# A hybrid attention and convolution step on one core: pacing of decode work, the engine of four weight halves, and two queue positions

## Chip, cores and metric

The kernel runs on one core of a Trainium2 chip. The metric is the device time of one execution in microseconds (us), and a median over several runs stands for a kernel. The engines are TensorE (PE, matmuls; PEld its weight loads), VectorE (DVE), ScalarE (ACT), GpSimd (POOL) and SyncE (SP, which here issues the DMAs). Each works through its own instructions in order and waits for others by semaphores.

## What is computed

One inference step of a two-layer trunk, for a prompt of 1024 rows of 1024 numbers and for 8 sample rows, which have their past K and V in 32 pages of 128 rows each. Everything is fp32.

```python
def ab_mix(x, ...):                         # layer 0
    q, k, v, g_a, u_b, g_b = split(x @ w_in)
    o_a = stick_breaking(q, [past; k], [past; v])   # sigmoid(z) * product of (1 - sigmoid) of later keys
    o_b = multiscale_pool(u_b) 
    return concat(o_a * silu(g_a), o_b * silu(g_b)) @ w_out

def c_mix(x, ...):                          # layer 1
    a, a_gate, gate = split(x @ w_in)
    c = depthwise_conv(a * sigmoid(a_gate), 31 taps)
    c = silu(layer_norm(c + b_dw))
    return (c * silu(gate)) @ w_out

x = layer_norm(ALPHA * x + ab_mix(x))       # then the same with c_mix
```

New K, V and the new pooling and convolution states are outputs too.

## The kernel before

**Numbers in two halves.** Each operand of a large matmul is split into a high part, rounded to the matmul's type (`whi`, `xh`, made by ACT), and the rest (`wlo`, `xl`, made by DVE or POOL as a subtraction). A product is three matmuls: high times high, low times high, high times low. `dma_w` (L198) loads a raw piece of a weight, `conv_w` (L203 to 211) makes its two halves: ACT copies at L205, and at L210 POOL subtracts, or DVE if the argument `eng` says so.

**Stages.** A setup transposes the inputs (L562) and the small weights (`setup_small`, L479: bias row, depthwise weights at L512, norm vectors). Then comes the input projection of layer 0, mixed with the attention of the prompt rows: 48 units (a head pair with a block of queries) with scores on PE, sigmoids on ACT, a scan and a product on DVE (L365 to 371), and the weighted sum on PE; the pooling groups are woven in between. Out layer 0 follows (`out_layer`, L1041): the output projection in 32 items of 24 matmuls, an item being a quarter of the columns (n4) for one block of 128 rows (tb), with the items (0, 0..3), (1, 0..3), (0, 4..7), (1, 4..7) first and the quarters 2 and 3 after. Each item is evacuated by DVE (L1067, L1071). A block that has all its quarters is normalized (L1009 DVE, L1025 ACT, L1026 POOL), and transposed by PE for the next layer (L1138). Layer 1 has its projection, the convolution (taps on DVE, ACT, POOL and PE), the conv norm and then out layer 1, again `out_layer`. The decode of V and the sample rows' small products run beside layer 1's work.

**The order** of the work of PE, ACT, DVE and POOL is the order in which the program is written; generators weave stages into each other. SP's order is made by the framework, which may move a DMA that depends on nothing. `decode_k` is a generator that scores the sample rows against their K pages. Each of its units loads two pages (L405), multiplies them with the query on POOL (three of four) or DVE (L417), and sums over a head on DVE (L409). After the 64 units of each half of the samples comes a tail: transposes and sigmoids (L429), a scan over 1024 columns (L437), a carry row (L441 to L451), scaling (L454), and transposes back (L463). `tick(n)` advances it by n steps. In attention a unit gets `TBASE + TSLOPE * (384 - n) / 384` ticks; what is left is spread over out layer 0, one tick after each item.

**Weights in out layer 0.** The first quarter's four pieces are ready before the layer; the second quarter's four are made in its first four steps, as `convs` says, with POOL for the even ones and DVE for the odd ones in layer 0 (L1059).

**Conv norm in layer 1.** `stats_3` (L1547) fills a queue, `midq`, in five steps `mid(0)` to `mid(4)` over the eight row blocks (1, 1, 2, 2 and 2 of them): PE broadcasts mean and scale by transposes (`mid_a`, L1569), and DVE subtracts and multiplies (`mid_b`, L1581), two operations of 128x1024 for a block. A SiLU group on ACT follows (`silus`, L1595), in two halves that are entries of the same queue, then the product with the gate (`mid_g`, L1602, DVE for blocks 3, 5 and 7, else POOL), and the split (`mid_c`: L195, L196). `midpop(EARLY)` takes three entries from the queue ahead of out layer 1; a `mid_g` takes entries until its SiLU group is out. `AT` places the rest: `mid_g(4)` at item (1, 1) of out layer 1, `mid_c(4)` at (1, 3). The sample row's norm stands beside it (L1230 to L1233, then PE's transposes L1208).

Of the kernel before, what the change touches and what calls it, by code (L numbers as in the profile page):

```python
# [65 lines left out]
WRB = 3  # L66
ETICK = 0.35
EDVE = (1, 2, 3, 0)
TBASE = 2.35
TSLOPE = 1.5  # L70
NHEADS = (0, 6, 6, 6, 6, 6, 6, 6)
SNY = 7
# [10 lines left out]
FASTB = (7,)  # L83
# [17 lines left out]
def kernel(  # L101
# [9 lines left out]
    pe, act, dve, gp, sp = nc.tensor, nc.scalar, nc.vector, nc.gpsimd, nc.sync  # L111
# [34 lines left out]
    def trp():  # L146
        return pz[0].tile([P, 512], F32, tag="zt", name="zt", bufs=NZT[0])
# [55 lines left out]
    def conv_w(raw, a, n, pool=None, eng=None, tags=("whi", "wlo"), bufs=4):  # L203
        hi = (pool or wpa).tile([P, a, n], F32R, tag=tags[0], name="whi", bufs=bufs)
        act.activation(out=hi, in_=raw, func=AF.Copy)  # L205
        if tags[1] == "kp":
            lo = pool.tile([P, 513], F32R, tag="kp", name="wlo", bufs=bufs)[:, 0:a * n].rearrange("p (k f) -> p k f", k=a)
        else:
            lo = (pool or wpa).tile([P, a, n], F32R, tag=tags[1], name="wlo", bufs=bufs)
        (eng or gp).tensor_tensor(out=lo, in0=raw, in1=hi.bitcast(F32), op=ALU.subtract)  # L210
        return hi, lo
# [259 lines left out]
    def tick(n):  # L471
        while n > 0 and queue:
            try:
                next(queue[0])
                n -= 1
            except StopIteration:
                queue.pop(0)
# [454 lines left out]
    queue.append(decode_k())  # L932
    small_gen = setup_small()
    fill = Filler(blocks_gen(blocks, CHUNKS, qw[0], when=WCONVA, lead=WLEAD))
    ecred = 0.0
    while ("v0", 2) not in fill.seen:
        fill.part()
        next(small_gen, None)
        if ("k0", 2) in fill.seen and (0, 0) not in SQ:
            prep(0, 0)  # L940
        ecred += ETICK
        tick(int(ecred))
        ecred -= int(ecred)
# [3 lines left out]
    for u in range(len(units) + 2):  # L947
        if u < len(units):
# [6 lines left out]
            fcred += fbase  # L955
            tcred += TBASE + TSLOPE * (384 - n) / 384.0
            z_a(u)
# [80 lines left out]
    def out_layer(w, first, ahead, X, gb, pool, finish, between, before=None, half=None, tail=None, lag=OLAG, fast0=FAST, wide=0, gps=()):  # L1038
        order = [(n4, tb) for t0 in (0, 4) for n4 in range(2) for tb in range(t0, t0 + 4)]
        for i in range(NTB + lag):  # L1040
            if i < NTB:  # L1041
                order.append((2, i))
            if i >= lag:
                order.append((3, i - lag))
        dmas = {0: (1, 3)} | {9 + i: (2, i) for i in range(4)} | {13 + i: (3, i) for i in range(4)}
        convs = {i: (1, i) for i in range(4)} | {12 + i: (2, i) for i in range(4)} | {16 + i: (3, i) for i in range(4)}
        raws, sts = {}, {}
        tiles = {0: first, 1: [], 2: [], 3: []}

        def fetch(q, i):  # L1050
            raws[q, i] = dma_quarter(w, q, i)

        for i in range(3):
            raws[1, i] = ahead[i]
        for s, (n4, tb) in enumerate(order):
            f0 = n4 * 256
            if s in convs:
                q, i = convs[s]
                tiles[q].append(conv_w(raws[q, i], 2, 256, pool if q % 2 else None, dve if q == 1 and i % 2 and fast0 is FASTB else None))  # L1059
            if s in dmas:  # L1060
                fetch(*dmas[s])
            if before is not None:
                before(n4, tb)
            o = (trp() if s < wide and s % 3 else acc())[:, 0:256]
            out_group(tiles[n4], o, tb, half)
            y = X[tb]
            dve.scalar_tensor_tensor(out=y[:, f0:f0 + 256], in0=y[:, f0:f0 + 256], scalar=ALPHA,  # L1067
                                     in1=o, op0=ALU.mult, op1=ALU.add)
            if n4 == 0:
                sts[tb] = pool.tile([P, 4, 6], F32, tag="st", name="st", bufs=NTB)  # L1070
            dve.bn_stats(sts[tb][:, n4, :], y[:, f0:f0 + 256])  # L1071
            if n4 == 3:
                fast = tb in fast0
                halves = (slice(0, 512), slice(512, 1024)) if tb >= 6 else (slice(0, 1024),)
                mv, rs = norm_s(pool, sts[tb])

                def app(y=y, mv=mv, rs=rs, tb=tb, fast=fast, halves=halves):
                    if fast and gps:
                        hs = (slice(0, 512), slice(512, 1024))
                        bs = [norm_fast(gb[0], y, mv, rs, h, i, gps) for i, h in enumerate(hs)]  # L1080
                        for h, b in zip(hs, bs):
                            b()
                            finish(tb, y, h)
                        return
                    norm_a(gb[0], y, mv, halves, gps)
                    for h in halves:
                        norm_b(gb[0], y, rs, fast, h)
                        finish(tb, y, h)
                defer((DTC if fast0 is FASTB else DTD)[tb], app)
            between(n4, tb)  # L1090
            point()
            if tail is not None:
                tail(n4, tb)
# [432 lines left out]
    MID = ((0, 1), (1, 2), (2, 4), (4, 6), (6, 8))  # L1526
# [19 lines left out]
        defer(4, stats_3)  # L1546

    def stats_3():
        for c in range(len(MID)):
            midq.append(lambda c=c: (mid_a(c), mid_b(c)))  # L1550
            if c < 2:
                silus(c)
        silus(2)
        reached.append(1)

    midq = []
# [6 lines left out]
    def mid_a(c):  # L1563
        a, b = MID[c]
        if c == 0:
            BC["wide"] = pz[0].tile([P, S], F32, tag="conv", name="rows", bufs=1)
        t = BC["wide"][:, c * 512:c * 512 + 512] if c < 2 else trp()
        for i, tb in enumerate(range(a, b)):
            pe.transpose(out=t[:, i * P:(i + 1) * P], in_=rmf[:, tb:tb + 1].broadcast_to([P, P]), identity=ident)  # L1569
            pe.transpose(out=t[:, 256 + i * P:256 + (i + 1) * P], in_=rvf[:, tb:tb + 1].broadcast_to([P, P]),  # L1570
                         identity=ident)
        BC[c] = t

    def mid_b(c):
        a, b = MID[c]
        t = BC[c]
        for i, tb in enumerate(range(a, b)):
            cc = C[:, tb]
            for o0, op in ((0, ALU.subtract), (256, ALU.mult)):
                bc = t[:, o0 + i * P:o0 + (i + 1) * P].rearrange("p (o c) -> p o c", o=1).broadcast_to([P, NK, P])  # L1580
                dve.tensor_tensor(out=cc, in0=cc, in1=bc, op=op)  # L1581
# [3 lines left out]
    def silus(c):  # L1585
        for i in range(SPLIT):
            midq.append(lambda i=i: mid_s(c, i))
# [71 lines left out]
    fill.part(1)  # L1659
    tick(1)  # L1660
    mid_c(1)
    for c in range(3, len(MID)):
        silus(c)
    midpop(EARLY)
    fill.part(1)
    tick(1)
# [36 lines left out]
```

## Time and profile before

| what | value |
|---|---|
| median of 3 runs | 1110.16 us (1109.91 to 1115.74) |
| profiled execution | 1110.31 us |
| its span in the profile | 1108.5 us |
| mean granted clock of PE | 0.972 |
| busy: PE, DVE, POOL, ACT | 1042.0, 833.3, 632.2, 493.4 us |

The profile shows one execution. A span is some 1.8 us shorter than the time of the execution, which has a start and an end around it. A row of a timeline gives the start, the busy time, the engine, the line, the operation with what it writes and reads, and in brackets how long the engine was idle before and what released it. A stage's row gives the busy time of each engine within it.

### The profile page before, as it was taken

How to read it: one execution, taken by the hardware profiler on the slowest of the kernel's cores; microseconds unless marked ns; L12 is line 12 of the kernel's file. 1: busy time of each engine (PE TensorE's matmuls, PEld its weight loads, DVE VectorE, ACT ScalarE, POOL GpSimd, SP SyncE). 2: the span in 40 equal slices, each digit the busy share in tenths (PEclk: the TensorE clock that was granted, in tenths of full speed). 3: DMA queues.
4: the chain of work that ended last, by engine and by line, in shares of the span. 5: the costliest groups of instructions: out<-in, count | busy, mean ns of one | idle time of the engine just before them, and what ended most of it. 6: DMA issues, size and time to landing. Idle time of an engine off the chain costs nothing.

```text
span 1108.5 us, 19858 instructions
## 1 busy us (share of the span) xinstructions
PE 1042.0 (94%) x6804; PEld 840.1 (76%) x6804; DVE 833.3 (75%) x982; ACT 493.4 (45%) x933; POOL 632.2 (57%) x488
## 2 busy tenths in 40 slices
PE   8899998999999989979988999999999899799996
PEld 7897887888888878979986666566666466678786
DVE  3368899899689988698874699999999960584246
ACT  5245665665766647601143244534543412462111
POOL 3266858567276878568765266757764612342135
PEclk9999999999999989989988999999999999889998
DMA  8577857865457776478425786877687678386933
GB/s 268 171 205 228 253 181 214 257 207 176 131 158 230 243 217 217 151 263 267 155 100 177 218 262 214 267 241 232 208 263 235 205 244 266 111 271 217 321 108 135
DMA packets 179350, 235.20 MB, mean 212 GB/s; under 512 B 15434, under 2 KB 95955, under 8 KB 179225
## 3 DMA queue, kind: packets, MB, share of 16 engines
q1 hardware_dynamic: 179249, 233.94, 67.0%
q8 instruction: 53, 0.87, 0.3%
q14 instruction: 48, 0.39, 0.1%
HBM read 212.60 MB, written 16.14 MB: 206 GB/s over the span
## 4 chain that ended last, share of the span: by engine, by line
PE 51%; POOL 7%; DVE 6%; DMA 5%; issue 2%; ACT 2%; SPq 2%; POOLq 0%; DVEq 0%; ACTq 0%
PE acc L225 10%; PE acc L227 9%; PE acc L226 9%; PE qv L1163 6%; DMA kt<-in_cache_k_dram 3%; POOL kt L417 2%; PE acc L1034 2%; PE acc L1036 2%; PE acc L1035 2%; DVE conv L1581 2%; PE zt L1034 1%; POOL wlo L210 1%; DVE xl L196 1%; PE qv L1199 1%; PE zt L1035 1%
## 5 line engine op out<-in xcount | busy, mean ns | idle before, releaser
L225 PE MATMUL acc<-xh,whi 128*128 128x384 f32 (+2 forms) x960 | 360.3, 375 | 1.9 <-DVE hbt L705 1.4
L227 PE MATMUL acc<-xl,whi 128*128 128x384 f32 (+2 forms) x960 | 339.3, 353 | 0.5 <-DVE xl L196 0.5
L226 PE MATMUL acc<-xh,wlo 128*128 128x384 f32 (+2 forms) x960 | 338.8, 353 | 0.0
L417 POOL TENSOR_TENSOR kt<-kt,qbs 128x1024 f32<-128x1024 f32 x96 | 237.8, 2487 | 79.0 <-DMA kt<-in_cache_k_dram 58.8
L210 POOL TENSOR_TENSOR wlo<-wraw,whi 128x512 fp32r<-128x512 f32 x122 | 163.6, 1345 | 176.6 <-ACT whi L205 154.0
L1385 DVE SCALAR_TENSOR_TENSOR conv_acc<-hbuf,wdwT,conv_acc 128x1024 f32<-128x1024 f32 x196 | 252.8, 1290 | 6.8
L225 PEld LDWEIGHTS acc<-xh,whi 128*128 128x128 f32 x960 | 183.0, 191 | 68.5 <-issue 27.2
L227 PEld LDWEIGHTS acc<-xl,whi 128*128 128x128 f32 x960 | 182.8, 190 | 18.4 <-DVE xl L196 0.9
L226 PEld LDWEIGHTS acc<-xh,wlo 128*128 128x128 f32 x960 | 183.4, 191 | 15.8
L409 DVE TENSOR_REDUCE zw<-kt 128x16 f32<-128x1024 f32 x128 | 152.9, 1211 | 28.0 <-POOL kt L417 23.0
L1375 POOL TENSOR_TENSOR conv<-conv,tap 128x512 f32<-128x512 f32 x84 | 105.9, 1293 | 15.5 <-ACT tap L1372 15.5
L205 ACT ACTIVATE whi<-wraw 128x512 fp32r<-128x512 f32 x126 | 77.6, 625 | 71.9 <-DMA wraw<-in_w_out_ab_dram 55.8
L1034 PE MATMUL acc<-whi,xh 128*128 128x256 f32 x352 | 103.9, 295 | 0.0
L1036 PE MATMUL acc<-whi,xl 128*128 128x256 f32 x352 | 101.0, 287 | 2.2 <-DVE xl L196 2.2
L1035 PE MATMUL acc<-wlo,xh 128*128 128x256 f32 x352 | 100.9, 287 | 0.6 <-POOL wlo L210 0.6
L365 DVE TENSOR_TENSOR_SCAN kp<-kp,zt 128x512 f32<-128x512 f32 (+3 forms) x96 | 92.5, 964 | 6.1 <-ACT zt L361 6.1
L1372 ACT ACTIVATE tap<-hbuf,wdwT 128x512 f32<-128x512 f32 x84 | 59.8, 721 | 46.1 <-POOL conv L1375 37.7
L1163 PE MATMUL qv<-vt,zw 128*32 128x512 f32 x512 | 74.5, 603 | 3.1 <-DMA vt<-in_cache_v_dram 3.1
L360 ACT ACTIVATE kp<-zt,nbiash 128x512 f32<-128x512 f32 (+3 forms) x96 | 55.8, 581 | 46.0 <-PE zt L823 24.5
L1034 PEld LDWEIGHTS acc<-whi,xh 128*128 128x128 f32 x352 | 68.5, 194 | 8.3 <-issue 7.8
L1036 PEld LDWEIGHTS acc<-whi,xl 128*128 128x128 f32 x352 | 68.5, 195 | 2.4 <-DVE xl L196 2.4
L1035 PEld LDWEIGHTS acc<-wlo,xh 128*128 128x128 f32 x352 | 68.5, 195 | 1.1 <-POOL wlo L210 1.0
(286 smaller groups left out, 1501.7 us busy)
## 6 DMA issues: line engine op xcount, KB each, us to landing
kt<-in_cache_k_dram SPq DMA_DIRECT2D x256, 256.0 KB
vt<-in_cache_v_dram SPq DMA_DIRECT2D x256, 256.0 KB
wraw<-in_w_in_c_dram SPq DMA_DIRECT2D x48, 256.0 KB
vt<-in_w_in_c_dram SPq DMA_DIRECT2D x48, 256.0 KB
wraw<-in_w_in_ab_dram SPq DMA_DIRECT2D x46, 256.0 KB
xt<-in_x_prompt_dram SPq DMA_DIRECT2D x8, 512.0 KB
wraw<-in_w_out_ab_dram SPq DMA_DIRECT2D x16, 256.0 KB
xres<-in_x_prompt_dram SPq DMA_DIRECT2D x8, 512.0 KB
```

Of the source, the lines that this page charges most:

```text
L210: (eng or gp).tensor_tensor(out=lo, in0=raw, in1=hi.bitcast(F32), op=ALU.subtract)
L225: pe.matmul(o, hi[:, k % 4, :], xh, start=(k == 0), stop=False)
L226: pe.matmul(o, lo[:, k % 4, :], xh, start=False, stop=False)
L227: pe.matmul(o, hi[:, k % 4, :], xl, start=False, stop=(k == NK - 1))
L409: dve.tensor_reduce(out=seg[:, j // 8, j % 8:j % 8 + 2, bi * 8:bi * 8 + 8], in_=kts.pop(s - KLAG - 1).rearrange("p a (h d) -> p a h d", d=DH),
L417: eng.tensor_tensor(out=kt, in0=kt, in1=qrow[b], op=ALU.mult)
L1034: pe.matmul(o, XH[:, k, cs], hi[:, k % 2, :], start=(k == 0), stop=False)
L1035: pe.matmul(o, XH[:, k, cs], lo[:, k % 2, :], start=False, stop=False)
L1036: pe.matmul(o, XL[:, k, cs], hi[:, k % 2, :], start=False, stop=(k == NK - 1))
L1163: pe.matmul(pv[32 * bi:32 * bi + 32, :], Z[:, j % 8 * 4 + j // 8, :], vts[bi], start=(j == 0), stop=(j == NPG - 1), tile_position=(0, 32 * ...
L1375: gp.tensor_tensor(out=ch, in0=ch, in1=tcs(t), op=ALU.add)
L1385: dve.scalar_tensor_tensor(out=part[1], in0=hb[:, j:j + S], scalar=w, in1=part[1], op0=ALU.mult, op1=ALU.add)
```

## The change

There are four edits. `TBASE` rises from 2.35 to 2.6. In the setup, the second and third advance of `setup_small` are left out, so that its later parts come two fill parts later. In out layer 0, POOL makes all low halves of the second quarter. In the conv norm, `mid(4)` is no longer queued with the others but behind the SiLU group 3.

```diff
--- before.py
+++ after.py
@@ -66,7 +66,7 @@
 WRB = 3
 ETICK = 0.35
 EDVE = (1, 2, 3, 0)
-TBASE = 2.35
+TBASE = 2.6
 TSLOPE = 1.5
 NHEADS = (0, 6, 6, 6, 6, 6, 6, 6)
 SNY = 7
@@ -932,10 +932,12 @@
     queue.append(decode_k())
     small_gen = setup_small()
     fill = Filler(blocks_gen(blocks, CHUNKS, qw[0], when=WCONVA, lead=WLEAD))
-    ecred = 0.0
+    ecred, early = 0.0, 0
     while ("v0", 2) not in fill.seen:
         fill.part()
-        next(small_gen, None)
+        early += 1
+        if early == 1 or early > 3:
+            next(small_gen, None)
         if ("k0", 2) in fill.seen and (0, 0) not in SQ:
             prep(0, 0)
         ecred += ETICK
@@ -1056,7 +1058,7 @@
             f0 = n4 * 256
             if s in convs:
                 q, i = convs[s]
-                tiles[q].append(conv_w(raws[q, i], 2, 256, pool if q % 2 else None, dve if q == 1 and i % 2 and fast0 is FASTB else None))
+                tiles[q].append(conv_w(raws[q, i], 2, 256, pool if q % 2 else None))
             if s in dmas:
                 fetch(*dmas[s])
             if before is not None:
@@ -1546,7 +1548,7 @@
         defer(4, stats_3)
 
     def stats_3():
-        for c in range(len(MID)):
+        for c in range(len(MID) - 1):
             midq.append(lambda c=c: (mid_a(c), mid_b(c)))
             if c < 2:
                 silus(c)
@@ -1659,8 +1661,9 @@
     fill.part(1)
     tick(1)
     mid_c(1)
-    for c in range(3, len(MID)):
-        silus(c)
+    silus(3)
+    midq.append(lambda: (mid_a(4), mid_b(4)))
+    silus(4)
     midpop(EARLY)
     fill.part(1)
     tick(1)
```

POOL at the start of out layer 0, behind the split of the pooled part; L210 makes the low halves of the second quarter (one row for each piece), L417 multiplies pages of K for the decode. Before:

```order
L196 TENSOR_TENSOR xl<-hs,xh 128x4x128 x4
L210 TENSOR_TENSOR wlo<-wraw,whi 128x512
L417 TENSOR_TENSOR kt<-kt,qbs 128x1024 x2
L210 TENSOR_TENSOR wlo<-wraw,whi 128x512
L417 TENSOR_TENSOR kt<-kt,qbs 128x1024 x7
```

and with the change:

```order
L196 TENSOR_TENSOR xl<-hs,xh 128x4x128 x4
L210 TENSOR_TENSOR wlo<-wraw,whi 128x512
L417 TENSOR_TENSOR kt<-kt,qbs 128x1024
L210 TENSOR_TENSOR wlo<-wraw,whi 128x512
L417 TENSOR_TENSOR kt<-kt,qbs 128x1024
L210 TENSOR_TENSOR wlo<-wraw,whi 128x512
L417 TENSOR_TENSOR kt<-kt,qbs 128x1024
L210 TENSOR_TENSOR wlo<-wraw,whi 128x512
L417 TENSOR_TENSOR kt<-kt,qbs 128x1024 x6
```

The second and fourth piece, which were on DVE, now stand on POOL, with one multiplication of K between each two.

DVE in out layer 0, around the scan of the decode tail (L437); L1067 and L1071 (L1069 and L1073 in the changed file) evacuate an item, L999, L1009 and L196 belong to the normalization and the split of finished blocks. Before:

```order
L1067 SCALAR_TENSOR_TENSOR xres<-xres,acc 128x256
L1071 BN_STATS st<-xres 128x6
L999 BN_AGGR mv<-st 128x2
L437 SCALAR_TENSOR_TENSOR kpd<-kpd 128x1024
L196 TENSOR_TENSOR xl<-zt,xh 128x4x128 x2
L1009 SCALAR_TENSOR_TENSOR xres<-xres,mv,o 128x512
L1009 SCALAR_TENSOR_TENSOR xres<-xres,mv,qv 128x512
L1067 SCALAR_TENSOR_TENSOR xres<-xres,acc 128x256
L1071 BN_STATS st<-xres 128x6
```

and with the change:

```order
L1069 SCALAR_TENSOR_TENSOR xres<-xres,acc 128x256
L1073 BN_STATS st<-xres 128x6
L1069 SCALAR_TENSOR_TENSOR xres<-xres,acc 128x256
L1073 BN_STATS st<-xres 128x6
L437 SCALAR_TENSOR_TENSOR kpd<-kpd 128x1024
L1069 SCALAR_TENSOR_TENSOR xres<-xres,acc 128x256
L1073 BN_STATS st<-xres 128x6
L1069 SCALAR_TENSOR_TENSOR xres<-xres,acc 128x256
L1073 BN_STATS st<-xres 128x6
```

The scan now stands among items of the middle of the layer, ahead of the first normalization.

DVE in out layer 1, at items (1, 1) to (1, 3); L1581 (L1583) is the conv norm's `mid_b`, L1602 (L1604) the product with the gate, L1223 to L1233 (L1225 to L1235) the sample row's norm. Before:

```order
L1223 TENSOR_SCALAR sA<-sA,zt 128x256
L1224 TENSOR_TENSOR sB<-sA 128x256
L1225 TENSOR_REDUCE small<-sB 128x1
L1602 TENSOR_TENSOR conv<-conv,gate 128x1024
L1067 SCALAR_TENSOR_TENSOR conv<-conv,zt 128x256
L1071 BN_STATS st<-conv 128x6
L1067 SCALAR_TENSOR_TENSOR conv<-conv,acc 128x256
L1071 BN_STATS st<-conv 128x6
L196 TENSOR_TENSOR xl<-conv,xh 128x8x128 x2
L1230 TENSOR_SCALAR small<-zt 128x1
L1232 SCALAR_TENSOR_TENSOR sA<-sA,small 128x256
L1233 TENSOR_TENSOR sA<-sA 128x256
```

and with the change:

```order
L1225 TENSOR_SCALAR sA<-sA,zt 128x256
L1226 TENSOR_TENSOR sB<-sA 128x256
L1227 TENSOR_REDUCE small<-sB 128x1
L1583 TENSOR_TENSOR conv<-conv,zt 128x1024 x4
L1604 TENSOR_TENSOR conv<-conv,gate 128x1024
L1069 SCALAR_TENSOR_TENSOR conv<-conv,zt 128x256
L1073 BN_STATS st<-conv 128x6
L1069 SCALAR_TENSOR_TENSOR conv<-conv,acc 128x256
L1073 BN_STATS st<-conv 128x6
L196 TENSOR_TENSOR xl<-conv,xh 128x8x128 x2
L1232 TENSOR_SCALAR small<-zt 128x1
L1234 SCALAR_TENSOR_TENSOR sA<-sA,small 128x256
```

The four operations of `mid(4)` now stand just ahead of the product with the gate. On ACT the same edit puts half a SiLU group (x4) ahead of the gate accumulator's evacuation at the start of out layer 1; before:

```order
L1595 ACTIVATE conv<-conv,pvec 128x128 x8
L205 ACTIVATE whi<-wraw 128x512 x2
L195 ACTIVATE xh<-conv 128x8x128
L1463 ACTIVATE gate<-acc 128x4x128
L205 ACTIVATE whi<-wraw 128x512 x2
L1463 ACTIVATE gate<-acc 128x4x128
L1595 ACTIVATE conv<-conv,pvec 128x2x128 x8
```

and with the change:

```order
L1597 ACTIVATE conv<-conv,pvec 128x128 x8
L205 ACTIVATE whi<-wraw 128x512 x2
L195 ACTIVATE xh<-conv 128x8x128
L1597 ACTIVATE conv<-conv,pvec 128x2x128 x4
L1465 ACTIVATE gate<-acc 128x4x128
L205 ACTIVATE whi<-wraw 128x512 x2
L1465 ACTIVATE gate<-acc 128x4x128
L1597 ACTIVATE conv<-conv,pvec 128x2x128 x4
```

The group's second half now stands behind the second evacuation. SP's order changes in one place: the copy of the conv state (L1111), which stood within attention, now stands behind it, ahead of the first four loads of `w_out_ab` (L200).

## Rows read from the trace of the kernel before

**Rows 1.** Busy time by stage: us of stage, busy us (x instructions), granted clock, DMA share, GB/s.

```profile
100.00:460.00 360.00, 346.14 (x2481) 305.81 (x2480) 307.82 (x379) 226.09 (x469) 242.50 (x144) 0.99 0.67 206
...
475.75:490.24 14.49, 6.99 (x33) 6.49 (x31) 14.35 (x16) 0.63 (x1) 8.04 (x4) 0.65 0.89 302
550.00:600.00 50.00, 38.88 (x244) 35.53 (x243) 32.74 (x54) 22.01 (x34) 34.20 (x46) 0.86 0.38 131
600.00:940.00 340.00, 336.86 (x1655) 211.92 (x1654) 278.35 (x222) 133.31 (x216) 181.48 (x154) 0.99 0.75 234
```

**Rows 2.** PE's timeline, setup: start us, us, engine, line, operation, [idle before, releaser].

```profile
32.85 0.55 PE L512 MATMUL zt<-ident,wdw_n 31*128 31x31 f32 x4 [2.89 <-DMA wdw_n<-in_w_dw_dram]
33.33 0.69 PE L225 MATMUL acc<-xh,whi 128*128 128x384 f32 x1
...
35.42 3.24 PE L562 MATMUL zt<-ident,xt 128*128 128x128 f32 x24
```

**Rows 3.** DVE's groups by line, 100 to 460 us: busy, mean ns | idle before, releasers.

```profile
L409 DVE TENSOR_REDUCE zw<-kt 128x16 f32<-128x1024 f32 x91 | 108.4, 1212 | 19.1 <-POOL kt L417 14.3 <-DMA kt<-in_cache_k_dram 4.4
```

**Rows 4.** The K tile's instructions, POOL's row: min/median/max ns, first and last start.

```profile
L417 POOL TENSOR_TENSOR kt<-kt,qbs x96: 2342/2397/3421, 54.7 to 542.7; 128x1024 f32<-128x1024 f32 x96
```

**Rows 5.** SP's DMA issues in attention.

```profile
382.45 0.83 SPq L1111 DMA_DIRECT2D out_dram<-in_state_conv_dram  x1
```

**Rows 6.** Busy time by stage, around the copy (columns as in rows 1).

```profile
380.00:385.00 5.00, 5.00 (x38) 4.41 (x36) 4.97 (x6) 2.70 (x8) 5.00 (x4) 1.00 1.06 336
400.00:405.00 5.00, 5.00 (x19) 4.03 (x20) 4.90 (x6) 2.09 (x5) 4.64 (x5) 0.50 0.44 138
```

**Rows 7.** DVE's timeline in attention.

```profile
395.42 1.22 DVE L409 TENSOR_REDUCE zw<-kt 128x16 f32<-128x1024 f32 x1 [4.40 <-DMA kt<-in_cache_k_dram]
```

**Rows 8.** PE's timeline in attention.

```profile
397.87 1.00 PE L713 MATMUL zt<-hbt,wpool 128*128 128x264 f32 x2 [3.83 <-DVE hbt L705]
```

**Rows 9.** PE's timeline at the start of out layer 0.

```profile
482.03 0.58 PE L1035 MATMUL zt<-wlo,xh 128*128 128x256 f32 x1 [6.02 <-DVE wlo L210]
...
486.44 0.58 PE L1035 MATMUL zt<-wlo,xh 128*128 128x256 f32 x1 [1.49 <-DVE wlo L210]
```

**Rows 10.** DVE's timeline at the start of out layer 0.

```profile
479.82 2.15 DVE L210 TENSOR_TENSOR wlo<-wraw,whi 128x512 fp32r<-128x512 f32 x1
...
485.71 0.68 DVE L210 TENSOR_TENSOR wlo<-wraw,whi 128x512 fp32r<-128x512 f32 x1
```

**Rows 11.** POOL's timeline at the start of out layer 0.

```profile
477.40 1.71 POOL L210 TENSOR_TENSOR wlo<-wraw,whi 128x512 fp32r<-128x512 f32 x1
```

**Rows 12.** PE's timeline at the end of out layer 0.

```profile
575.34 1.72 PE L1138 MATMUL zt<-ident,xres 128*128 128x128 f32 x8 [4.12 <-POOL xres L1026]
...
592.06 1.70 PE L463 MATMUL zt<-ident,zw 128*128 128x128 f32 x8 [2.56 <-DVE xl L196]
```

**Rows 13.** DVE's timeline at the end of out layer 0.

```profile
564.88 4.25 DVE L437 TENSOR_TENSOR_SCAN kpd<-kpd 128x1024 f32<-128x1024 f32 x1
```

**Rows 14.** PE's timeline in out layer 1.

```profile
968.69 0.28 PE L1034 MATMUL acc<-whi,xh 128*128 128x256 f32 x1
...
982.12 0.58 PE L1036 MATMUL acc<-whi,xl 128*128 128x256 f32 x1 [2.22 <-DVE xl L196]
...
1007.02 0.38 PE L1208 MATMUL zt<-ident,sA 128*128 128x128 f32 x2
```

**Rows 15.** DVE's timeline in out layer 1.

```profile
965.39 14.40 DVE L1581 TENSOR_TENSOR conv<-conv,zt 128x1024 f32<-128x1024 f32 x12
...
996.52 1.22 DVE L1602 TENSOR_TENSOR conv<-conv,gate 128x1024 f32<-128x1024 f32 x1
...
1001.14 2.36 DVE L196 TENSOR_TENSOR xl<-conv,xh 128x1024 fp32r<-128x1024 f32 x2
```

**Rows 16.** ACT's timeline in out layer 1.

```profile
970.28 4.05 ACT L1595 ACTIVATE conv<-conv,pvec 128x256 f32<-128x256 f32 x8 [0.79 <-DVE conv L1581]
```

**Rows 17.** POOL's timeline in out layer 1.

```profile
996.57 3.44 POOL L1602 TENSOR_TENSOR conv<-conv,gate 128x1024 f32<-128x1024 f32 x1 [4.81 <-ACT conv L1595]
```

## The prediction

> **What bounds the kernel now.** I read the busy time by stage first [rows 1]. Attention (100 to 460 us) keeps TensorE (PE) busy for 346.14 of 360 us and VectorE (DVE) for 307.82; the long stage from 600 to 940 us keeps PE busy for 336.86 of 340. A microsecond won on PE before 600 us is therefore carried to the end, unless something in that long stage was late by itself, and nothing there shows it. The two holes are the start of out layer 0 (475.75 to 490.24 us: PE busy 6.99 of 14.49 us, granted clock 0.65, which is a mean over the 1.2 and 2.4 GHz levels) and its end (550 to 600 us: 38.88 of 50 us, clock 0.86). Then I read the timelines of the engines around each place that the change touches, to see which wait ended last there. The sum is made against the profiled execution's 1110.31 us; the median of the runs shown is 1110.16, so both can be taken as one base.
>
> **The change, part by part** (minus is a gain).
>
> *Small conv weights later.* PE waited 2.89 us for the small conv weights' DMA and went on at 32.85 us; the six projection matmuls between 33.33 us and the transposes at 35.42 us then took 0.35 us each [rows 2]. Two parts later these transposes stand behind the 24 input transposes (3.24 us), and the DMA has landed by then. The wait goes (2.89), and something of the slow stretch behind it. The next thing that can be late is the low half of the inputs, which needs those 24 transposes. I take -3.5; between -1.5 (the low half takes the wait over) and -4.5.
>
> *Decode paced up.* The change raises the base rate by 0.25 in 48 attention units: 12 units of decode work move from out layer 0 into attention. Each is two 256 KB loads, one reduction on DVE (1.21 us, [rows 3]) and one multiplication, three of four on GpSimd (POOL; median 2.40 us, [rows 4]) and the fourth on DVE, which I price like the reduction over the same 128x1024. On DVE that is 12 x 1.21 + 3 x 1.21 = 18.2 us, on POOL 9 x 2.40 = 21.6 us. The stage has 360 - 307.82 = 52 us of DVE not busy, but part of it is DVE waiting for POOL's multiplication, 14.3 us [rows 3]. If all the added work finds a gap, the cost is 0; if none does, PE's order is pushed by DVE's 18.2 less PE's own idle 360 - 346.14 = 13.9, some 4, and at worst (its gaps lie elsewhere) by three quarters of it, about 14. I take +5, near the lower end, since most of the stage has PE as the later engine. Range 0 to +14.
>
> *A copy that moves with it.* The order on the queue of SyncE (SP) changes too: the DRAM-to-DRAM copy of the conv state, issued at 382.45 us [rows 5], moves behind all of the attention stage, ahead of the first loads of w_out0. In the five microseconds in which it was issued, the DMA share was 1.06 [rows 6]; behind it DVE waited 4.40 us for a page of K [rows 7], PE waited 3.83 us for DVE [rows 8], and the granted clock was 0.50 in 400 to 405 us [rows 6]. Without the copy the stall could vanish, 3.83 us and about 2.5 of slow clock; but with decode further ahead, another wait for K may stand there. I take -3.5, range -6.5 to 0. At its new place PE still has other work, and the loads of the first quarter are not yet wanted.
>
> *Low weights on GpSimd.* At the start of out layer 0 PE waited 6.02 and then 1.49 us for the low halves that DVE makes [rows 9]. DVE took 2.15 us for the first and 0.68 us for the second, and stood in a long queue [rows 10]; POOL's own took 1.71 us [rows 11]. After the change POOL makes all four with one K multiplication between each two, as the order ahead shows. Counting from POOL's row at 477.40 us backwards, the second tile is ready near 476, the third near 480, the fourth near 484, and PE waits for the third and the fourth, some 3.4 + 3.0 = 6.4 us instead of 7.5: a gain of 1 to 2. I take -1.5; range -4 (a full clock comes back as well) to +2 (POOL's multiplications run long beside DVE).
> Against this edit speaks a rule of the Trainium skill ("GPSIMD Engine Reference", section "4.1 Engine selection"): elementwise work on two inputs belongs on VectorE, with GpSimd about twice as slow. The rows agree as to the lone instruction (1.71 against 0.68 us), but not for the one that held PE longest (2.15 us on DVE). By the rule alone this term would be a loss of some 2 us, and the sum -2 us instead of -5.5.
>
> *End of out layer 0.* With 12 units fewer to do, the tail of the decode work (transposes, scan, carry, scaling) leaves the end of the layer for its middle, where each step has two or three items of 24 matmuls between it and the next. Before, PE waited 4.12 us there for a normalized row block and 2.56 us ahead of the last decode transposes [rows 12], two waits of several; the first is held up by the 4.25 us scan on DVE [rows 13]. All of it together is PE's idle time, 50 - 38.88 = 11.1 us, and the slow clock, 38.88 x (1 - 0.86) = 5.4 us: 16.5 us at most. I take -13, since a few waits belong to the normalization itself; range -7 (only the waits on the tail, with their slow clock) to -16.
>
> *Last statistics step of the conv norm.* At the start of out layer 1 PE waited 2.22 us [rows 14] for what stood behind twelve 1.2 us operations in a row on DVE (14.40 us from 965.39, [rows 15]). Now four of the twelve are put into step (1,1). Two prices stand against that. First, the queue's early pops now take the first half of a SiLU group instead of them, and ACT's evacuation of a gate accumulator, which frees what PE's first product at 968.69 us [rows 14] needs, and two weight copies come behind it. That SiLU waits for DVE's first four operations, to 965.39 + 4.8 = 970.2, and takes half of 4.05 us [rows 16]: PE idles from 968.7 to about 975, and only part of it comes back where the old stall was. Second, in step (1,1) the chain becomes serial: DVE's four operations stand where its product with the gate began at 996.52 [rows 15] and take 4.8 us to 1001.3, the SiLU 4.05 us to 1005.4, the product on POOL 3.44 us [rows 17] to 1008.8, the cast some 1 us, then DVE's low halves and the sample row's norm behind them, which took 1007.02 - 1001.14 = 5.9 us from the start of the low halves to PE's transposes [rows 14, 15]. DVE waits for the SiLU in the middle and can do none of it earlier. That gives PE's transposes near 1015.5 instead of 1007.02: +8.5, in which the first loss is contained, and some +2.5 for two more transposes' place and a slow clock behind the wait. I take +11 for the edit; range +4 (the SiLU finds its way early and POOL's product takes its shorter time) to +14.
>
> **Sum:** -3.5 + 5 - 3.5 - 1.5 - 13 + 11 = -5.5 on 1110.31, so 1104.8 us.
>
> **The rivals.**
> (a) *The late statistics hide.* If the sample row's norm has slack in step (1,1), the last edit costs +4 or nothing, and the sum is -12.5 to -16.5: 1094 to 1098 us. For it: PE has full items queued. Against: its transposes stand in PE's fixed order, at a fixed item.
> (b) *The end of out layer 0 gains half.* The normalization's own waits take over when the decode tail is gone; the term is -7 and the sum +0.5: about 1111 us. For it: the 4.12 us wait names POOL's normalization, not the scan.
> (c) *DVE becomes the bound of attention.* The decisive place is the K loop: once DVE's 18.2 us fall into stretches where it has no gap, each unit delays the scan that PE's next product waits for. That is +14 for the term, and with the copy's gain eaten by the next wait for K the sum is -3.5 + 14 + 0 - 1.5 - 13 + 11 = +7: about 1117 us, slower. It decides from about +13 for the two terms of attention together. For it: DVE is busy 86% of the stage. Against: PE is busier still.
> (d) *The move to POOL costs instead of gaining.* If POOL's three K multiplications ahead of the fourth tile take the longest time seen, 3.42 us instead of 2.40 [rows 4], that tile is ready near 487, behind the 486.44 us of before [rows 9], with the slow clock running as much longer: +2 instead of -1.5, sum -2, about 1108 us. For it: both engines work on large operands there; against: those long times are few. The rule from the Trainium skill's "GPSIMD Engine Reference", "4.1 Engine selection", is on the side of (d).
>
> **How the numbers follow.** The forecast's case has a chance of 0.37, (a) 0.24, (b) 0.13, (c) 0.20, (d) 0.06. A difference of 0.5% is 5.6 us, about what a measurement of this kernel can tell from none; the forecast lies right at it, so its 0.37 is split, 0.20 faster and 0.17 same. Faster: 0.20 + 0.24 = 0.44. Same: 0.17 + 0.13 + 0.06 = 0.36. Slower: 0.20. The range reaches from the middle of (a) to near the middle of (c), 1095 to 1117 us, and leaves out the far halves of both.
>
> **What would show it.** Right: no wait of PE at the small conv weights; no wait over 3 us on low weights made by DVE at the start of out layer 0, but two of about 3 us on POOL's; the scan of the decode tail in the middle of out layer 0 and PE busy over 45 of the last 50 us of the layer; in out layer 1 a wait of PE of 6 us at its first items and one at the sample row's transposes. The prediction is wrong if attention ends over 8 us later or earlier than the terms say, or if PE shows no wait at those transposes.

## The result, and the profile after

The changed kernel takes 1143.54 us (median of 4 runs, 1139.56 to 1145.82), against 1111.91 us for the kernel before on the same chip: a ratio of 1.0291, with a 95% interval of 1.0259 to 1.0324. That is slower, far outside the range of 1095 to 1117 us. The profiled execution took 1142.64 us, its span 1140.8 us, 32.3 us more than before.

Where the time went follows from the start of the same PE instruction in the two traces (after less before, worked out from both timelines):

| place | shift, us | what the stretch up to it cost |
|---|---|---|
| first scores of attention | -3.6 | setup: -3.6 |
| first item of out layer 0 (463.63 before, 491.51 after) | +27.9 | attention: +31.5 |
| first V work of layer 1 (610.66, 628.72) | +18.1 | out layer 0: -9.8 |
| conv norm's first transposes (943.52, 961.32) | +17.8 | layer 1: -0.3 |
| out layer 1, item (1, 2) and on to the sample row's transposes | +23.0, then +32.4 | last statistics step: +14.6 |
| last matmul | +32.0 | -0.4 |

The setup, out layer 0 and the last statistics step came within 5 us of their terms (-3.5, -14.5 and +11). Attention did not: +1.5 us were forecast for it (pace and copy together), and it lost 31.5. The stage from 60 us to the first item of out layer 0, before:

```profile
60.00:463.63 403.63, 387.43 (x2738) 344.27 (x2737) 338.92 (x415) 248.78 (x520) 273.81 (x159) 0.99 0.68 206
```

and after:

```profile
60.00:491.51 431.51, 394.02 (x2717) 346.50 (x2716) 354.25 (x426) 247.98 (x518) 293.26 (x167) 0.96 0.67 206
```

The columns are those of [rows 1]. The stage is 27.9 us longer. PE's idle time rose from 16.2 to 37.5 us (stage less busy), 21.3 us, and its busy time by 6.6 us with the same work, at a mean granted clock of 0.96 instead of 0.99. DVE is busy for 15.3 us longer, with 10 reductions more in this window (two of the twelve added units stand ahead of 60 us, since the setup is earlier). The waits of these reductions, DVE's group by line over the same stage, answer to [rows 3]. Before:

```profile
L409 DVE TENSOR_REDUCE zw<-kt 128x16 f32<-128x1024 f32 x103 | 122.7, 1212 | 24.2 <-POOL kt L417 19.4 <-DMA kt<-in_cache_k_dram 4.4
```

and after:

```profile
L409 DVE TENSOR_REDUCE zw<-kt 128x16 f32<-128x1024 f32 x113 | 134.4, 1213 | 30.6 <-POOL kt L417 29.7 <-DMA kt<-in_cache_k_dram 0.2
```

The wait for POOL grew by 10.3 us, and the 4.4 us of waits for loads of K fell to 0.2. So DVE's queue holds 15.3 + 6.4 = 21.7 us more of work and waiting, and PE's idle time grew by 21.3. What the wait looks like is seen at PE's longest stall after, 7.04 us. PE, DVE and POOL there, each from its timeline:

```profile
396.36 0.77 PE L815 MATMUL zt<-km,qh 128*128 128x512 f32 x1 [7.04 <-issue]
```

```profile
383.01 1.22 DVE L409 TENSOR_REDUCE zw<-kt 128x16 f32<-128x1024 f32 x1 [1.23 <-POOL kt L417]
386.60 1.22 DVE L409 TENSOR_REDUCE zw<-kt 128x16 f32<-128x1024 f32 x1 [2.37 <-POOL kt L417]
388.96 1.22 DVE L409 TENSOR_REDUCE zw<-kt 128x16 f32<-128x1024 f32 x1 [1.14 <-POOL kt L417]
390.10 2.23 DVE L417 TENSOR_TENSOR kt<-kt,qbs 128x1024 f32<-128x1024 f32 x1
392.25 2.56 DVE L794 TENSOR_TENSOR ql<-qo,qh 128x256 fp32r<-128x256 f32 x1
394.73 0.94 DVE L365 TENSOR_TENSOR_SCAN kp<-kp,zt 128x384 f32<-128x384 f32 x1
395.70 0.56 DVE L369 TENSOR_TENSOR sg<-zt,kp 128x384 f32<-128x384 f32 x1
```

```profile
384.18 10.35 POOL L417 TENSOR_TENSOR kt<-kt,qbs 128x1024 f32<-128x1024 f32 x4
```

POOL multiplies four pages in a row for 10.35 us. DVE's three reductions each wait for one of them. Behind them in DVE's order stand a multiplication of its own, L794 (the low half of queries that are needed later), and only then the scan and the product (L365, L369) of the scores that PE had made before. The trace names no releaser for PE here ("issue"), but PE goes on at 396.36, 0.10 us after L369 ends. It goes on as closely behind an L369 at 92.45 and 187.76 us in the kernel before, where this wait took 2.09 and 1.94 us, and at 397.74 us with the pace edit alone (6.85 us). The code says why: attention has five tiles for scores and transposes (`NZT = [5]`). The two scores of the unit before, two tiles of transposes and the first score of this unit take all five, and the second score needs the first of them again, which L369 is the last to read. So PE waits for DVE's scan and product, and these stand behind reductions that wait for POOL. PE's next longest wait after, 5.05 us at 196.19 us, names another operation of DVE (L611).

### The profile page after: what moved, and what is told of

The parts are those of the page before. It is cut to its first block, busy times and chain, and to the rows that moved or that the text cites. A ratio compares the mean times of both kernels' runs of the same rounds, so it can differ in the third digit from the quotient of the medians.

```text
span 1140.8 us, 19840 instructions
## 1 busy us (share of the span) xinstructions
PE 1048.5 (92%) x6804; PEld 841.9 (74%) x6804; DVE 830.7 (73%) x980; ACT 493.6 (43%) x933; POOL 633.9 (56%) x490
## 4 chain that ended last, share of the span: by engine, by line
PE 47%; DVE 8%; POOL 7%; issue 6%; DMA 5%; ACT 2%; SPq 1%; POOLq 0%; DVEq 0%; ACTq 0%
PE acc L225 9%; PE acc L227 8%; PE acc L226 8%; PE qv L1165 6%; DMA kt<-in_cache_k_dram 2%; PE acc L1036 2%; PE acc L1038 2%; PE acc L1037 2%; DVE xl L196 2%; POOL kt L417 1%; POOL wlo L210 1%; PE qv L1201 1%; PE zt L1036 1%; POOL xres L1028 1%; DVE zw L409 1%
## 5 line engine op out<-in xcount | busy, mean ns | idle before, releaser
L417 POOL TENSOR_TENSOR kt<-kt,qbs 128x1024 f32<-128x1024 f32 x96 | 237.0, 2477 | 74.1 <-DMA kt<-in_cache_k_dram 63.3
L210 POOL TENSOR_TENSOR wlo<-wraw,whi 128x512 fp32r<-128x512 f32 x124 | 169.9, 1375 | 181.8 <-ACT whi L205 172.9
L409 DVE TENSOR_REDUCE zw<-kt 128x16 f32<-128x1024 f32 x128 | 152.5, 1212 | 33.3 <-POOL kt L417 32.3
L365 DVE TENSOR_TENSOR_SCAN kp<-kp,zt 128x512 f32<-128x512 f32 (+3 forms) x96 | 92.6, 964 | 7.0 <-ACT zt L361 7.0
```

Source lines behind the costliest of these rows:

```text
L409: dve.tensor_reduce(out=seg[:, j // 8, j % 8:j % 8 + 2, bi * 8:bi * 8 + 8], in_=kts.pop(s - KLAG - 1).rearrange("p a (h d) -> p a h d", d=DH),
L417: eng.tensor_tensor(out=kt, in0=kt, in1=qrow[b], op=ALU.mult)
```

## Experiments

Ratios are to the kernel before on the same chip, with 95% intervals. A difference between two experiments is one of medians; the kernel before had medians from 1108.2 to 1111.9 us beside them, so such a difference is good to some 4 us. What is said of a stage comes from one trace of each kernel.

### Each edit by itself

**e1_pace_only**

```diff
-TBASE = 2.35
+TBASE = 2.6
```

> The kernel before with the pace edit alone (TBASE 2.6). Theory P (the added decode units fall into stretches of attention where VectorE has no gap, and push TensorE's order): attention is longer by 28 to 33 us, out layer 0 shorter by about 9, in all 18 to 24 us slower than before, near 1132. Rival S (the setup edit shifts the phase between loads of K and attention, and that makes the loss): within 6 us of before.

Measured 1133.31 us, 1.0228 (1.0178 to 1.0279). Attention ended 28.7 us later than before, out layer 0 gave 8 back. Theory P holds as to the place, and rival S falls. The stage in its trace, and the group of reductions in it:

```profile
60.00:492.30 432.30, 396.21 (x2732) 348.87 (x2730) 354.29 (x428) 249.15 (x521) 293.46 (x168) 0.96 0.67 207
```

```profile
L409 DVE TENSOR_REDUCE zw<-kt 128x16 f32<-128x1024 f32 x115 | 136.5, 1212 | 29.2 <-POOL kt L417 28.5
```

PE's idle time is 36.1 us, 19.9 more than before, and its busy time 8.8 more: the two make up the 28.7.

**e2_undo_pace** is the changed kernel with `TBASE = 2.35`.

> The changed kernel with the pace back at 2.35. Theory P: setup -3.5, low weights -1 to -2, last statistics step +12 to +13, in all 7 to 9 us slower than before, near 1119. Rival S: attention keeps most of its loss, 1135 or more.

Measured 1123.83 us, 1.0103 (1.0056 to 1.0150), some 11 us slower than before, where 7 to 9 were expected. In its trace attention ends 2.0 us earlier than before and the last matmul is 15.4 later: the loss that is left lies in out layer 1.

**e3_mid_only**

```diff
-        for c in range(len(MID)):
+        for c in range(len(MID) - 1):
...
-    for c in range(3, len(MID)):
-        silus(c)
+    silus(3)
+    midq.append(lambda: (mid_a(4), mid_b(4)))
+    silus(4)
```

> The kernel before with the last statistics step moved, and nothing else. If the change's traces show this edit alone (out layer 1's first items and the transposes of the sample row later by 12.9 us together), it is 11 to 14 us slower than before; if that loss needed the other edits, under 6.

Measured 1124.37 us, 1.0127 (1.0084 to 1.0170). The edit costs its 14 us without the others: 4.7 us at the first items of out layer 1, the rest at the sample row's transposes.

**e4_setup_low** is the kernel before with the counter `early` in the setup and without DVE in `conv_w`.

> The kernel before with the setup edit and the low weights on GpSimd. Theory P: -3.5 and -1 to -2, so 4 to 6 us faster than before, near 1105. Rival S: attention longer by 20 us or more. If the low weights cost instead of gaining (the page's rule), -1 to -2 in all.

Measured 1107.88 us, 0.9986 (0.9960 to 1.0011): no difference that these runs can tell, and less than the 4 to 6 us expected. In its trace the setup gains, attention loses a part of that again, and at the first item of out layer 0 only 1.8 us are left.

**e14_low_only** has the `conv_w` edit alone.

> The kernel before with the low weights edit alone. By the traces of the changed kernel PE's waits there are 5.8 us instead of 7.5: 1 to 3 us faster at the start of out layer 0, and within 3 us of before in all. By the page's rule 2 us slower.

Measured 1110.36 us, 1.0000 (0.9971 to 1.0028). PE's waits there fall from 7.5 to 5.3 us in the trace. In the kernel's time the interval reaches 3 us to either side, so it can tell neither the gain of 1.5 us that was forecast nor a loss of 2.

### What an added decode unit costs in attention

**e12_pace_down** sets `TBASE = 2.1`, 12 units fewer than before.

> The kernel before with the pace at 2.1: 12 units of decode work moved out of attention into out layer 0. Theory Q: attention is shorter by 5 to 15 us (the waits shrink less than they grew), out layer 0 longer by 10 to 15 us: within 8 us of before. If attention was just under a threshold, it gains nothing there and the kernel is 10 to 15 us slower.

Measured 1123.63 us, 1.0110 (1.0074 to 1.0147). Attention is 12.3 us shorter, as expected; out layer 0 is 23 us longer, where 10 to 15 were expected. So the pace of before stands at a bend: the 12 units below it cost attention 1.0 us each (12.3 / 12), the 12 above it 2.4 us each (28.7 / 12). The stage in its trace:

```profile
60.00:451.34 391.34, 383.48 (x2735) 341.46 (x2733) 315.94 (x398) 249.51 (x520) 247.04 (x150) 1.00 0.64 196
```

From this pace to that of before DVE's queue gains 26.0 us (23.0 of work, 3.0 of waits for POOL and loads), and PE's idle time only 8.3 (from 7.9 to 16.2). From before to e1 it gains 20.4, and PE's idle time 19.9. So a part of DVE's idle time did take in added units, up to about the pace of before.

**e5_pool_half** (the pace edit, and half of POOL's products left out)

```diff
-                    eng.tensor_tensor(out=kt, in0=kt, in1=qrow[b], op=ALU.mult)
+                    kh = kt[:, 0:1, :] if eng is gp else kt
+                    qh_ = qrow[b][:, 0:1, :] if eng is gp else qrow[b]
+                    eng.tensor_tensor(out=kh, in0=kh, in1=qh_, op=ALU.mult)
```

> Pace 2.6 alone, with GpSimd's multiplication of K done for one of the two pages only (the products of the other page are left out). Theory Q (VectorE's reduction waits in its queue for GpSimd's multiplication when several decode units come together, and what attention needs stands behind it): the wait falls away, attention gives back 20 to 30 us of the 29 it lost, near 1105 or below. Rival V (VectorE's own work has no gap): attention keeps most of the loss, 1125 or more.

Measured 1102.04 us, 0.9934 (0.9914 to 0.9954), 31 us below the pace alone. Attention gives back 25.9 of its 28.7 us in the trace; the rest comes from out layer 0, where half of POOL's products is left out too. The loads of K are all there, so they are not what held attention. DVE's reductions and multiplications do the same work as in e1 (115 reductions), and the waits are down to 12.2 us:

```profile
L409 DVE TENSOR_REDUCE zw<-kt 128x16 f32<-128x1024 f32 x115 | 136.0, 1212 | 12.2 <-POOL kt L419 11.2 <-DMA kt<-in_cache_k_dram 0.2
```

**e6_dve_half** (the pace edit, and half of each sum left out)

```diff
-in_=kts.pop(s - KLAG - 1).rearrange("p a (h d) -> p a h d", d=DH),
+in_=kts.pop(s - KLAG - 1).rearrange("p a (h d) -> p a h d", d=DH)[:, :, :, 0:32],
```

> Pace 2.6 alone, with VectorE's reduction over half of each head only (the other half of the sums is left out): 0.6 us instead of 1.2 for each unit, the same waits. Rival V: attention gives back 20 us or more, near 1108 or below. Theory Q: under 12 us back, 1120 or more.

Measured 1115.79 us, 1.0048 (1.0025 to 1.0072), 17.5 us below the pace alone: between the two theories. Attention gives back 12.5 us. DVE does 61 us less of sums, but waits twice as long, most of it for POOL:

```profile
L409 DVE TENSOR_REDUCE zw<-kt 128x16 f32<-128x512 f32 x114 | 75.7, 680 | 58.7 <-POOL kt L417 47.5 <-DMA kt<-in_cache_k_dram 10.4 <-issue 0.2
```

A cheaper reduction reaches its wait earlier; POOL's row of multiplications sets when it gets through. DVE's work and waits in the stage together are 361 us here, no more than the 363 before, and yet PE idles for 27.2 us instead of 16.2: where the waits stand counts, and not their sum with the work alone.

**e10_pace_split** (the pace edit, `KMOD = 2`, `KPOOL = 1`: DVE does every second multiplication)

> Pace 2.6 alone, with the multiplications of K shared half and half by GpSimd and VectorE (before: three to one). Theory Q: VectorE's waits for GpSimd fall under 20 us and a part of the loss comes back, 5 to 15 us below the 1133 of the pace alone. Rival V: VectorE's further 39 us of multiplications in all push attention out, 1140 or more.

Measured 1153.29 us, 1.0375 (1.0341 to 1.0409), 20 us above the pace alone. The waits are nearly gone, and 29 multiplications more, at 1.7 us each, stand in DVE's queue in their place:

```profile
L409 DVE TENSOR_REDUCE zw<-kt 128x16 f32<-128x1024 f32 x115 | 137.1, 1213 | 6.7 <-POOL kt L417 4.5 <-DMA kt<-in_cache_k_dram 1.0
L417 DVE TENSOR_TENSOR kt<-kt,qbs 128x1024 f32<-128x1024 f32 x58 | 99.9, 1723 | 0.0
```

Here rival V is right. Neither theory holds alone: what DVE does and what it waits for both hold up attention's operations behind them.

**e8_lag_pace** (the pace edit, `KLAG = 1`, the reduction two steps behind the multiplication)

> Pace 2.6 alone, with the multiplication of a unit's K one step earlier (one step behind its load instead of two), so that VectorE's reduction comes two steps behind it instead of one, with the same buffers. Theory Q: VectorE's waits for GpSimd fall from about 30 us to under 12, and 10 to 20 us of the loss come back, if GpSimd's waits for loads of K do not grow as much. Rival V: no gain, 1130 or more.

Measured 1146.71 us, 1.0327 (1.0284 to 1.0370), 13 us above the pace alone. The wait for POOL fell to 12.1 us as expected, but a load now has one step less, and DVE's own multiplications, which waited for nothing in the kernel before, wait 32.0 us for it:

```profile
L409 DVE TENSOR_REDUCE zw<-kt 128x16 f32<-128x1024 f32 x115 | 135.8, 1210 | 12.1 <-POOL kt L417 12.1
L417 DVE TENSOR_TENSOR kt<-kt,qbs 128x1024 f32<-128x1024 f32 x29 | 46.3, 1596 | 32.0 <-DMA kt<-in_cache_k_dram 32.0
```

A further buffer, which would let both be early, was not tried.

**e13_pace_spread** (the pace edit, steps at three points of a unit)

```diff
-        tick((k + 1) // 2)
+        ks = [(k + 2 - i) // 3 for i in range(3)]
+        tick(ks[0])
         slot(1)
         fill.part(fs[1])
+        tick(ks[1])
         slot(2)
-        tick(k // 2)
         fill.part(fs[2])
+        tick(ks[2])
```

> Pace 2.6 alone, with the decode steps of an attention unit placed at three points instead of two, so that two steps rarely stand together. If the loss comes from steps that stand together (VectorE waiting for the multiplication issued just before), attention gives back 10 to 20 us of 29 and VectorE's waits for GpSimd fall from 28 to under 15. If it is the sum of VectorE's work and GpSimd's in the stage, the waits move and the time stays within 6 us of 1133.

Measured 1122.33 us, 1.0114 (1.0069 to 1.0160), 11 us below the pace alone. The waits fell from 29.2 to 23.6 us, less than expected, and attention ended 21.9 us later than before instead of 28.7. So placing the steps apart takes away about a quarter of the loss in attention. How the rest divides into the waits that are left and the added work is not shown. In out layer 0 this version gains more than the pace alone; why is not shown.

### The statistics step and the copy

**e11_mid_early2** (e3 with `EARLY = 2`)

> The last statistics step moved, with two early pops instead of three, so that no half SiLU group stands ahead of the gate accumulator's evacuation. If that half group makes the first loss (+4.7 us at the first items of out layer 1) and the serial chain at step (1,1) the second (+8 to +9), the first goes and the second stays: 8 to 10 us slower than before instead of 14. If the chain's length sets the time by itself, still 13 to 15.

Measured 1117.58 us, 1.0065 (1.0037 to 1.0094), some 7 us slower than before, where 8 to 10 were expected. The first loss is gone: at out layer 1's fourth item PE is 2.5 us earlier than before. The second stays, with the same wait as in the changed kernel:

```profile
1013.60 0.69 PE L1208 MATMUL zt<-ident,sA 128*128 128x128 f32 x2 [6.61 <-DVE sA L1233]
```

**e7_copy_only**

```diff
         if n4 == 0 and tb == 4:
             sp.dma_start(pool_sample[0, :, 0:PS_ - 1, :], state_pool[0, :, 1:PS_, :])
+        if n4 == 2 and tb == 0:
             sp.dma_start(conv_sample[0, :, 0:KS - 1, :], state_conv[0, :, 1:KS, :])
```

> The kernel before with the copy of the conv state written later, so that it leaves attention, nothing else. If the copy made the stall near 395 us of the kernel before, that stall is under 1 us and the kernel 4 to 6 us faster; if another transfer made it, no difference.

Measured 1102.72 us, 0.9915 (0.9884 to 0.9947), a larger gain than the 4 to 6 us expected, though the stall is not under 1 us. The framework issued the copy at 415.01 us, still in attention, and put some loads of K in another order beside it. DVE's 4.40 us wait for a page of K is gone; of PE's stall, 2.53 us are left:

```profile
399.57 0.45 PE L225 MATMUL acc<-xh,whi 128*128 128x384 f32 x1 [2.53 <-DVE hbt L705]
```

Its profiled execution was the slowest of its six (1109.55 us; the others took 1099.61 to 1105.30), so the whole gain of 9 us can't be shown in the trace; how much of it is the copy and how much the order of the loads stays open.

**e9_copy_setup** (e7 and the setup edit)

> The kernel before with the copy of the conv state written later and the setup edit. If the two gains are there side by side (the copy alone measured 0.9915 of before; setup 2 to 3.5 us by the traces), 8 to 12 us faster than before, near 1099, and faster than both kernels; if the setup's gain is lost again inside attention, 5 to 9 us.

Measured 1098.60 us, 0.9900 (0.9858 to 0.9941): the fastest version, faster than both kernels by some 11 and 45 us.

**e15_copy_setup_low** (e9 and the `conv_w` edit)

> The copy written later, the setup edit and the low weights together: the best version as far as known. 0 to 3 us below the 1098.6 of the copy and the setup edit, so 1095.5 to 1099, faster than both kernels.

Measured 1104.82 us, 0.9930 (0.9902 to 0.9958). The 1095.5 to 1099 us expected were missed. Its interval and that of e9 overlap; the low weights add nothing that can be told.

**e16_copy_setup_spread** (e9 and the three points of e13, at the pace of before)

> The copy written later, the setup edit and the decode steps at three points, at the pace of before (2.35). If steps that stand together hold attention at this pace too, 5 to 10 us below the 1098.6 without the spread; if the two points were not what cost, within 4 us of it.

Measured 1104.55 us, 0.9963 (0.9936 to 0.9990). At the pace of before the spread gives no gain. It came out 6 us above e9, past the 4 expected for no effect; the two intervals just overlap, so whether it costs anything is not shown.

## Why the prediction was wrong, point by point

**Decode paced up: the step that failed.** The prediction took +5 (range 0 to +14) on the ground that DVE had 52 us not busy in the stage and that "most of the stage has PE as the later engine". The runs show 28.7 us in e1, with whatever the copy gave already in it. The prediction had named the sign: attention ends 27.9 us later, where its terms gave -2.0. Three things were mis-sized. The gaps of DVE were not there for the new units: the 15.4 us of work that e1 adds to DVE, and some 5 us more of waiting, came out as 19.9 us of PE's idle time, almost one for one. (The twelve units below the pace of before did find gaps, as e12 shows: a third of their work and waits came out.) The ground given, that PE is the later engine in most of the stage, no longer holds above it. The wait of a reduction for the multiplication issued one step earlier was read in [rows 3], but taken only as a part of the gaps, not as something that grows. And the slow clock that follows PE's stalls had no term: 8.8 us in e1. Rival (c) had the mechanism and the sign, down to the scan that PE's next product waits for; its price, half of what was measured, came from the same bound.

**The copy.** PE's 3.83 us wait behind it fell to 1.66 us (1.26 in e1), about as forecast, but its price can't be told from that of the added units. Between two scans of DVE on either side of it (386.77 and 405.72 us before), the changed kernel gains 2.8 us and e1 6.2 us against before, where -3.5 with bounds of -6.5 and 0 had been taken. Counted from the scan at 380.16 us they gain only 0.4 and 1.6, since both lose just ahead of it, and behind it they lose 3 and 4 us more. e7, which moves the copy less far, is 9 us faster.

**Setup.** Right: -3.6 us by the first scores of attention, -3.5 forecast, and PE's 2.89 us wait is gone. Over all traces the first scores start at 66.5 to 67.8 us in the six kernels with this edit and at 68.1 to 71.4 us in the twelve without it, 3.2 us apart in the mean. But attention takes a part of it back in e4, which the sum had not allowed for.

**Low weights on POOL.** The waits came about as forecast, on the third and fourth piece, with a short one on the second. PE after:

```profile
504.70 0.39 PE L1037 MATMUL zt<-wlo,xh 128*128 128x256 f32 x1 [0.77 <-POOL wlo L210]
...
508.69 0.50 PE L1037 MATMUL zt<-wlo,xh 128*128 128x256 f32 x1 [3.00 <-POOL wlo L210]
...
512.24 0.58 PE L1037 MATMUL zt<-wlo,xh 128*128 128x256 f32 x1 [1.98 <-POOL wlo L210]
```

Together 5.8 us, where [rows 9] show 7.5. The Trainium skill's "GPSIMD Engine Reference", "4.1 Engine selection", puts elementwise work on two inputs on VectorE, with GpSimd about twice as slow. By that the edit would have cost; in the traces of this kernel and of e14 PE's waits got shorter instead, and rival (d) falls. That DVE's piece stood behind other work of DVE is the likely reason, which no run isolates. The 1.7 us are too little for the time in e14 to tell.

**End of out layer 0.** The tail did leave the end, and its waits of [rows 12] with it; the layer gained 9.8 us against 14.5 forecast with the low weights. The term of -13 was too large: of the last 50 us, up to 620 us, PE is still idle for some 6.5, and busy for 43.53 where over 45 had been the sign. What is left is the normalization of the last row block on DVE and the slow clock behind it, as rival (b) said, with a smaller part:

```profile
609.60 1.94 PE L1140 MATMUL zt<-ident,xres 128*128 128x128 f32 x8 [4.26 <-DVE xres L1021]
```

```profile
570.00:620.00 50.00, 43.53 (x309) 40.26 (x308) 30.46 (x58) 18.79 (x28) 31.39 (x44) 0.93 0.37 126
605.00:615.00 10.00, 5.74 (x20) 4.68 (x19) 6.49 (x10) 3.38 (x6) 9.43 (x17) 0.66 0.63 208
```

**Last statistics step.** The mechanism was right in both parts, and rival (a) falls; +11 was forecast, 14.6 measured (14 by e3). PE, DVE and POOL after:

```profile
991.22 0.58 PE L1036 MATMUL acc<-whi,xh 128*128 128x256 f32 x1 [4.55 <-ACT whi L205]
...
1037.73 0.69 PE L1210 MATMUL zt<-ident,sA 128*128 128x128 f32 x2 [6.60 <-DVE sA L1235]
```

```profile
1019.15 4.85 DVE L1583 TENSOR_TENSOR conv<-conv,zt 128x1024 f32<-128x1024 f32 x4
1028.12 1.23 DVE L1604 TENSOR_TENSOR conv<-conv,gate 128x1024 f32<-128x1024 f32 x1 [4.12 <-ACT conv L1597]
...
1032.70 2.36 DVE L196 TENSOR_TENSOR xl<-conv,xh 128x1024 fp32r<-128x1024 f32 x2 [1.78 <-ACT xh L195]
```

```profile
1028.16 3.42 POOL L1604 TENSOR_TENSOR conv<-conv,gate 128x1024 f32<-128x1024 f32 x1 [18.86 <-ACT conv L1597]
```

The serial chain is the one of the prediction (4.85, 4.05 on ACT, 3.42 on POOL). The size was off since the first loss was held to be contained in the second: the chain in item (1, 1) stands behind the evacuation of PE's items, so the 5 us of the first items (23.0 - 17.8) shifted it, and the second loss came on top. e11 bears this out: there the first is gone and the second stays.

**The sum.** With the measured terms, -3.6 + 31.5 - 9.8 - 0.3 + 14.6 - 0.4 = 32.0 us, next to the 32.3 between the two profiled executions. Of the 37.5 us between that and the forecast's -5.5, attention holds 30.0. Without the pace edit (e2) the kernel is 11 us slower by the ratio and 15.4 us in its trace, where the other terms give +9 with the copy left in place, -3.5 - 1.5 + 14; the interval of e2, 6 to 17 us, holds both.

## What to carry to other kernels

An engine's idle share in a stage is not free time to its end: ask at which point of its in-order queue the added work stands, what it waits for there, and what stands behind it. Here the units below the pace of before cost PE's idle time a third of their work and waits, and the units above it nearly all, with a lower mean clock besides. A pace that is spread over two stages has to be measured on both sides: the run at 2.1 alone, where 12 units cost out layer 0 23 us and attention 12, would have spoken for more decode in attention, and the run at 2.6 shows that it is wrong.

## What was not expected of the hardware

The clock's share in the loss: in e1 PE's busy time rose by 8.8 us with the same instructions, against 19.9 us of idle time and at a mean granted clock of 0.96 instead of 0.99, so each microsecond of stall brought nearly half of another. In the changed kernel it was a third (6.6 against 21.3). One further number: the 128x256 subtraction L794 took 2.56 us at 392.25 us after, beside a multiplication on POOL, and 0.42 us at 385.78 us in the kernel before, where POOL had nothing running.
